# A 31-tap convolution's running sums: two channel tiles in PSUM on VectorE, the third on GpSimd, and softmax probabilities scaled on GpSimd

## The chip, the cores and the metric

The kernel runs on one core of a Trainium2 chip. The metric is the time of one execution in microseconds of the device, as the median of several runs. The core's engines run side by side, each through its own list of instructions in order: TensorE (PE in the profile; PEld is its weight load), VectorE (DVE), ScalarE (ACT), GpSimd (POOL) and SyncE (SP), which here starts the transfers.

## The reference

Two blocks of a network follow each other on 256 positions of 1024 channels, all in float32. The first has two layers with a mixer, a cross-attention to a memory of 256 rows and an MLP. The second has two layers of this form:

```python
h = x + 0.5 * swiglu(rms_norm_2(x, ffn1_norm[l]), ...)
p = rms_norm_2(h, mix_norm[l]) @ w_in[l]
u_conv, q, k, v, q_mem = jnp.split(p, splits, axis=-1)
y_conv = conv_module(u_conv, ...)        # gate, 31-tap causal convolution per channel, layer norm, silu
y_swa  = sliding_window_attention(q, k, v, swa_sinks[l])
y_mem  = memory_attention(qm, mk, mv)
h = h + jnp.concatenate([y_conv, y_swa, y_mem], axis=-1) @ w_out[l]
h = h + 0.5 * swiglu(rms_norm_2(h, ffn2_norm[l]), ...)
```

The convolution has 384 channels, each with its own 31 weights and a bias: the output at a position is the bias plus the sum over taps `j` of weight `j` times the input `30 - j` positions earlier. Every attention takes a softmax: exponentials, their sum, and each probability divided by that sum.

## The kernel before

Activations lie with 128 positions or 128 channels on the partitions. Matrix products run in float32 as three passes (`mm3`, L325 to L327): each weight tile is loaded by a transfer into `raw`, rounded by ScalarE into `hi` (L303), and the rest `raw - hi` is made by VectorE as `lo` (L304). Products add up in PSUM tiles of 128x512, which one engine at a time works on: three of tag `acc`, two of `tp` (transposes) and three of `sm` (scores).

`mixer` (L1209) is the middle of a layer of the second block. It is written as Python generators that `weave` (L388) interleaves: `conv_proj` makes the gated input of the convolution and puts it, with the channels on the partitions, into `yp` (three channel tiles `g`, 256 positions each and a border of zeros); `kv`, `qk_proj` and `vm_proj` make keys, queries and values, with rotary factors at L1195 and L1203; `mem` and `swa` are the two attentions; `taps` is the convolution, woven tap by tap with that chain; `ln` (L1427) follows it with a layer norm and the activation. `out_proj` (L479) multiplies everything with `w_out`, the convolution's three channel tiles last (the order 6, 7, 3, 4, 5, 0, 1, 2 at L1477).

In `taps` before, VectorE takes taps 0 to 16 of all three channel tiles: one multiply with bias at L1393 and sixteen multiply-adds at L1404 for each tile, in place in the SBUF tile `cv`. ScalarE takes the products of taps 17 to 30 (L1397, L1412), and GpSimd adds them in `cv2` (L1416), thirteen adds for each tile. At the end VectorE adds `cv` and `cv2` (L1420). The number of taps on VectorE is `ND` (L1565).

`softmax_ps` (L508) serves the cross-attention of the first block (L907) and both attentions of the mixer: VectorE takes the maximum (L512) and its negative times a factor (L515), ScalarE the exponentials with their sum (L525), VectorE the reciprocal (L534) and then, head by head, the scaling of the probabilities (L536). The probabilities are then transposed by TensorE (L383) into PSUM, copied by ScalarE (L909, L1335 or L1369) and multiplied with the values (L914, L1340 or L1374). A softmax of the cross-attention or of the memory attention has two heads of 128x256; of the sliding attention four and two heads of 128x128 for the first half of the positions, and three times two heads of 128x256 for the second. The factors of norms are powers taken on GpSimd (L424).

The order of each engine's instructions is not the order of the code. `list_schedule` (L128) plans it once, when the kernel is built: it takes estimated lengths (`length`, L102), the dependences and the number of buffers per tag, and gives each engine the earliest instruction in program order among those that are ready. Buffers of a tag are given out in program order. GpSimd's estimate is the same for an add and for a scaling.

## Time and profile before

| what | value |
|---|---|
| median of 3 runs | 1706.66 us (1706.2 to 1707.57) |
| the profiled execution | 1706.04 us |
| its span, first to last instruction | 1704.3 us |
| TensorE busy | 1656.1 us, 97% |
| VectorE busy | 1128.3 us, 66% |
| ScalarE busy | 941.7 us, 55% |
| GpSimd busy | 155.5 us, 9% |

The span is the profile's own clock from the first to the last instruction; the execution's time has 1.7 us around it. The two mixers of the second block, in which the convolution runs, lie at about 905 to 1019 us and 1395 to 1512 us of the span; the cross-attentions of the first block at about 160 to 215 and 460 to 520 us. A duration in a row reaches to the end of the write, so that two neighbours on one engine overlap a little: the distance from start to start is shorter than the duration.

### The profile page before, as it was taken

The numbers are of one execution on the slowest core, as the hardware profiler recorded it, in microseconds if no ns is written. First come the engines' busy times: TensorE is split into PE (matmuls) and PEld (weight loads), VectorE is DVE, ScalarE is ACT, GpSimd is POOL, SyncE is SP. The second block draws the span as 40 slices with busy tenths as digits, with TensorE's granted clock in tenths as the row PEclk, the third lists the DMA queues.
The fourth block names the chain that finished last, engine by engine and source line by source line (L and its number), as shares of the span: only waits on it lengthen the run. The fifth ranks groups of instructions, "written<-read, shape, count | busy, mean of one in ns | idle before, by whom it ended". The sixth has DMA issues, their size and how long they took to land.

```text
span 1704.3 us, 22757 instructions
## 1 busy us (share of the span) xinstructions
PE 1656.1 (97%) x8144; PEld 1399.0 (82%) x8144; DVE 1128.3 (66%) x1899; ACT 941.7 (55%) x1685; POOL 155.5 (9%) x185
## 2 busy tenths in 40 slices
PE   8999999999999999999999799999999998799998
PEld 7878888888888888888888578888888887588886
DVE  7876475556657558557558996556665559975454
ACT  7675564445666445545446674445654447664343
POOL 0120000000000000000002810000100006500000
PEclk9999999999999999999999799999999999799999
DMA  9536365565535565556455055646655554355552
GB/s 306 177 104 206 100 197 185 178 211 171 187 112 164 182 202 175 198 167 197 163 191 179 32 159 182 203 157 218 212 179 177 169 186 137 86 166 169 197 167 93
DMA packets 159393, 291.45 MB, mean 171 GB/s; under 512 B 11184, under 2 KB 36272, under 8 KB 159280
## 3 DMA queue, kind: packets, MB, share of 16 engines
q1 hardware_dynamic: 159280, 290.00, 52.6%
q8 instruction: 64, 1.05, 0.2%
q14 instruction: 49, 0.40, 0.1%
HBM read 288.91 MB, written 1.05 MB: 170 GB/s over the span
## 4 chain that ended last, share of the span: by engine, by line
PE 89%; DVE 7%; ACT 2%; issue 1%; DMA 1%; SPq 0%; POOL 0%; POOLq 0%; DVEq 0%; ACTq 0%
PE acc L327 27%; PE acc L326 27%; PE acc L325 27%; PE tp L383 4%; DVE big L1404 3%; DVE lo L304 1%; PE sm L914 1%; PE sm L901 1%; PE sm L383 1%; DVE st L555 0%; PE acc L622 0%; DVE t L536 0%; PE acc L620 0%; PE acc L621 0%; PE sm L1324 0%
## 5 line engine op out<-in xcount | busy, mean ns | idle before, releaser
L325 PE MATMUL acc<-hi,h 128*128 128x512 f32 (+1 forms) x2048 | 786.1, 384 | 1.2 <-ACT h L367 1.2
L326 PE MATMUL acc<-lo,h 128*128 128x512 f32 (+1 forms) x2048 | 783.6, 383 | 1.2 <-DVE lo L304 1.2
L327 PE MATMUL acc<-hi,h 128*128 128x512 f32 (+1 forms) x2048 | 784.5, 384 | 0.0
L304 DVE TENSOR_TENSOR lo<-raw,hi 128x1024 fp32r<-128x1024 f32 (+2 forms) x570 | 651.5, 1160 | 146.2 <-ACT hi L303 132.9
L303 ACT CAST hi<-raw 128x1024 fp32r<-128x1024 f32 (+2 forms) x570 | 564.8, 1005 | 275.0 <-PE acc L327 246.2
L325 PEld LDWEIGHTS acc<-hi,h 128*128 128x128 f32 x2048 | 385.8, 188 | 66.7 <-ACT h L367 2.1
L326 PEld LDWEIGHTS acc<-lo,h 128*128 128x128 f32 x2048 | 385.6, 188 | 65.8 <-DVE lo L304 1.8
L327 PEld LDWEIGHTS acc<-hi,h 128*128 128x128 f32 x2048 | 385.5, 188 | 64.0 <-issue 0.7
L424 POOL TENSOR_TENSOR st<-st,nhalf 128x1 f32<-128x1 f32 (+2 forms) x74 | 68.6, 929 | 1483.8 <-DVE st L429 1256.2
L367 ACT CAST h<-tp 128x512 fp32r<-128x512 f32 (+1 forms) x80 | 45.1, 563 | 151.7 <-PE tp L383 151.5
L477 DVE SCALAR_TENSOR_TENSOR x<-acc,st,x 128x512 f32<-128x512 f32 x48 | 35.9, 748 | 86.7 <-PE acc L327 86.3
L368 DVE TENSOR_TENSOR h<-tp,h 128x512 fp32r<-128x512 f32 (+1 forms) x80 | 52.9, 662 | 58.5 <-ACT h L367 58.3
L383 PE MATMUL tp<-ident,t 128*128 128x128 f32 x488 | 76.6, 275 | 13.1 <-DVE t L1157 5.9
L439 ACT ACTIVATE t<-x 128x512 f32<-128x512 f32 x56 | 35.6, 638 | 97.1 <-DVE x L477 76.7
L383 PEld LDWEIGHTS tp<-ident,t 128*128 128x128 f32 x488 | 60.2, 141 | 30.9 <-DVE t L1157 6.8
L1113 DVE TENSOR_TENSOR t<-acc,t 128x512 f32<-128x512 f32 (+1 forms) x48 | 30.9, 643 | 82.5 <-PE acc L327 82.5
L1416 POOL TENSOR_TENSOR big<-big,big 128x256 f32<-128x256 f32 x78 | 66.6, 882 | 5.1 <-ACT big L1412 5.1
L325 PE MATMUL acc<-hi,big 128*128 128x512 f32 x160 | 64.4, 403 | 0.0
L1110 ACT ACTIVATE t<-acc,st 128x512 f32<-128x512 f32 (+1 forms) x48 | 31.1, 649 | 60.0 <-PE acc L327 60.0
L326 PE MATMUL acc<-lo,big 128*128 128x512 f32 x160 | 63.6, 398 | 0.0
L1111 DVE SCALAR_TENSOR_TENSOR t<-t,acc 128x512 f32<-128x512 f32 (+1 forms) x48 | 30.7, 640 | 49.7 <-ACT t L1110 49.7
L327 PE MATMUL acc<-hi,big 128*128 128x512 f32 x160 | 63.5, 397 | 0.0
(237 smaller groups left out, 1193.0 us busy)
## 6 DMA issues: line engine op xcount, KB each, us to landing
raw<-in_ffn_w_dram SPq DMA_DIRECT2D x208, 512.0 KB, 5.1
raw<-in_mlp_w_dram SPq DMA_DIRECT2D x128, 512.0 KB, 4.8
raw<-in_ffn_w_dram SPq DMA_DIRECT2D x64, 384.0 KB, 4.1
raw<-in_xa_w_kv_dram SPq DMA_DIRECT2D x32, 512.0 KB, 5.2
raw<-in_ev_w_in_dram SPq DMA_DIRECT2D x20, 512.0 KB, 6.0
raw<-in_w_in_dram SPq DMA_DIRECT2D x24, 384.0 KB, 4.7
raw<-in_xa_w_q_dram SPq DMA_DIRECT2D x16, 512.0 KB, 5.1
raw<-in_xa_w_o_dram SPq DMA_DIRECT2D x16, 512.0 KB, 5.6
```

The costliest lines, as they stand in the source:

```text
L303: nc.scalar.copy(hi[:, :n], raw[:, :n])
L304: nc.vector.tensor_tensor(out=lo[:, :n], in0=raw[:, :n], in1=hi[:, :n].bitcast(F32), op=ALU.subtract)
L325: nc.tensor.matmul(ps, l[0], r[0], start=start, stop=False)
L326: nc.tensor.matmul(ps, l[0], r[1], start=False, stop=False)
L327: nc.tensor.matmul(ps, l[1], r[0], start=False, stop=stop)
L367: nc.scalar.copy(h, src)
L368: nc.vector.tensor_tensor(out=self.lo(k0, n, t), in0=src, in1=h.bitcast(F32), op=ALU.subtract)
L383: nc.tensor.transpose(dst[:, i * P : i * P + rows], s_, ident[:rows, :rows])
L424: nc.gpsimd.tensor_tensor(out=dst, in0=src, in1=nhalf[:, :n], op=ALU.pow)
L477: nc.vector.scalar_tensor_tensor(x_, ps, scale, x_, op0=ALU.mult, op1=ALU.add)
L1404: nc.vector.scalar_tensor_tensor(cv[:, g], yp[:, g, 2 + j : 258 + j], col(cw, 93 * l + 3 * j + g), cv[:, g], op0=ALU.mult, op1=ALU.add,)
L1416: nc.gpsimd.tensor_tensor(out=cv2[:, g], in0=cv2[:, g], in1=pj[:, g], op=ALU.add)
```

## The change

The convolution is shared out by channel tile in place of by tap. For channel tiles 0 and 1 all 31 taps run on VectorE, with the running sum in one PSUM tile `run` of tag `acc` (two tiles of 256 side by side); the last tap writes to `cv` in SBUF. For channel tile 2 ScalarE makes all 31 products (the first with the bias, straight into `cv`), and GpSimd adds thirty of them to `cv` in a row. Two products share a tile of tag `t2`, which also holds the softmaxes' tiles. The final add of VectorE is gone, and so is `ND`. In `softmax_ps` the scaling of the probabilities goes from VectorE to GpSimd. The lines after the change: L1406 first tap and L1410 other taps on VectorE, L1397 and L1401 products on ScalarE, L1402 adds on GpSimd, L536 scaling on GpSimd.

```diff
         for h in range(nh):
-            nc.vector.tensor_scalar(dst[:, h], dst[:, h], rc[:, h : h + 1], None, op0=ALU.mult)
+            nc.gpsimd.tensor_scalar(dst[:, h], dst[:, h], rc[:, h : h + 1], None, op0=ALU.mult)
...
         def taps(t):
-            cv = spare("m2hi0")
-            cv2 = spare("m2lo0")
-            for g in range(3):
-                nc.vector.tensor_scalar(
-                    cv[:, g], yp[:, g, 2:258], col(cw, 93 * l + g), col("conv_b_2", 3 * l + g),
-                    op0=ALU.mult, op1=ALU.add,
-                )
...
-                        nc.vector.scalar_tensor_tensor(
-                            cv[:, g], yp[:, g, 2 + j : 258 + j], col(cw, 93 * l + 3 * j + g),
-                            cv[:, g], op0=ALU.mult, op1=ALU.add,
-                        )
...
-            nc.vector.tensor_tensor(out=cv, in0=cv, in1=cv2, op=ALU.add)
+            cv = big()[:, 0:3]
+            run = c3(acc(), 256)
+            for j in range(31):
+                if j % 2 == 1:
+                    pj = c3(t2(), 256)
+                for g in range(3):
+                    w_ = col(cw, 93 * l + 3 * j + g)
+                    src = yp[:, g, 2 + j : 258 + j]
+                    if g == 2 and j == 0:
+                        nc.scalar.activation(
+                            cv[:, 2], src, AF.Identity, scale=w_, bias=col("conv_b_2", 3 * l + g)
+                        )
+                    elif g == 2:
+                        nc.scalar.activation(pj[:, j % 2], src, AF.Copy, scale=w_)
+                        nc.gpsimd.tensor_tensor(
+                            out=cv[:, 2], in0=cv[:, 2], in1=pj[:, j % 2], op=ALU.add
+                        )
+                    elif j == 0:
+                        nc.vector.tensor_scalar(
+                            run[:, g], src, w_, col("conv_b_2", 3 * l + g), op0=ALU.mult, op1=ALU.add
+                        )
+                    else:
+                        nc.vector.scalar_tensor_tensor(
+                            cv[:, g] if j == 30 else run[:, g], src, w_, run[:, g],
+                            op0=ALU.mult, op1=ALU.add,
+                        )
+                yield
             cvs.append(cv)
```

The planner moves instructions at three places that the prediction speaks of. The first is VectorE in the first mixer, at the softmaxes of the memory attention (`sm` scores, `t2` probabilities, `big_1733` is `cv`, `big_1694` is `yp`). Before:

```order
L534 RECIPROCAL st_1858_8739<-st_1857_8736 128x2
L1404 SCALAR_TENSOR_TENSOR big_1733_8260<-big_1694_8082,G_72,big_1733_8260 128x256
L555 TENSOR_SCALAR st_1849_8719<-st_1848_8717,st_1684_8051 128x4
L536 TENSOR_SCALAR t2_1854_8731<-t2_1854_8731,st_1858_8739 128x256 x2
L512 TENSOR_REDUCE st_1875_8846<-sm_1873_8842 128x2
L534 RECIPROCAL st_1869_8797<-st_1868_8794 128x2
L515 SCALAR_TENSOR_TENSOR st_1876_8848<-st_1875_8846,st_1849_8719 128x2
L536 TENSOR_SCALAR t2_1865_8789<-t2_1865_8789,st_1869_8797 128x256 x2
L1404 SCALAR_TENSOR_TENSOR big_1733_8260<-big_1694_8082,G_72,big_1733_8260 128x256 x6
L368 TENSOR_TENSOR h4_1862_8773<-sm_1853_8728,h4_1861_8772 128x128
L1404 SCALAR_TENSOR_TENSOR big_1733_8260<-big_1694_8082,G_72,big_1733_8260 128x256 x2
L368 TENSOR_TENSOR h4_1862_8773<-sm_1864_8786,h4_1861_8772 128x128
```

After the change (`acc_1734` is the running sum):

```order
L534 RECIPROCAL st_1855_8703<-st_1854_8700 128x2
L515 SCALAR_TENSOR_TENSOR st_1870_8779<-st_1869_8777,st_1846_8683 128x2
L1410 SCALAR_TENSOR_TENSOR acc_1734_8261<-big_1694_8082,G_72,acc_1734_8261 128x256 x2
L534 RECIPROCAL st_1865_8745<-st_1864_8742 128x2
L1410 SCALAR_TENSOR_TENSOR acc_1734_8261<-big_1694_8082,G_72,acc_1734_8261 128x256 x2
L534 RECIPROCAL st_1872_8784<-st_1871_8781 128x2
L1410 SCALAR_TENSOR_TENSOR acc_1734_8261<-big_1694_8082,G_72,acc_1734_8261 128x256 x9
L368 TENSOR_TENSOR h4_1858_8726<-sm_1850_8692,h4_1857_8725 128x128
L1410 SCALAR_TENSOR_TENSOR acc_1734_8261<-big_1694_8082,G_72,acc_1734_8261 128x256 x4
L1410 SCALAR_TENSOR_TENSOR big_1733_8260<-big_1694_8082,G_72,acc_1734_8261 128x256
L368 TENSOR_TENSOR h4_1858_8726<-sm_1860_8734,h4_1857_8725 128x128
L1410 SCALAR_TENSOR_TENSOR big_1733_8260<-big_1694_8082,G_72,acc_1734_8261 128x256
```

The scalings are gone from this list. Three reciprocals now stand close together, and behind them come the last fifteen multiply-adds of the convolution, two of which write to `cv`.

The second place is GpSimd at the end of the same mixer (`big_1734` was `cv2`, `st` are small columns). Before:

```order
L1416 TENSOR_TENSOR big_1734_8261<-big_1734_8261,big_1872_8835 128x256 x3
L1416 TENSOR_TENSOR big_1734_8261<-big_1734_8261,big_1879_8860 128x256 x3
L1223 MEMSET big_2661_12617 128x3x32
L424 TENSOR_TENSOR st_1940_9117<-st_1939_9115,nhalf_76 128x1
L424 TENSOR_TENSOR st_1951_9150<-st_1950_9148,nhalf_76 128x1
```

After the change:

```order
L1402 TENSOR_TENSOR big_1733_8260<-big_1733_8260,t2_1914_8984 128x256
L1402 TENSOR_TENSOR big_1733_8260<-big_1733_8260,t2_1915_9004 128x256
L536 TENSOR_SCALAR t2_1883_8853<-t2_1883_8853,st_1890_8879 128x128 x4
L536 TENSOR_SCALAR t2_1896_8915<-t2_1896_8915,st_1903_8935 128x128 x2
L1402 TENSOR_TENSOR big_1733_8260<-big_1733_8260,t2_1915_9004 128x256
L1223 MEMSET big_2663_12609 128x3x32
L1402 TENSOR_TENSOR big_1733_8260<-big_1733_8260,t2_1925_9043 128x256 x2
L536 TENSOR_SCALAR t2_1906_8960<-t2_1906_8960,st_1913_8980 128x256 x2
L536 TENSOR_SCALAR t2_1917_9010<-t2_1917_9010,st_1924_9030 128x256 x2
L536 TENSOR_SCALAR t2_1927_9059<-t2_1927_9059,st_1934_9079 128x256 x2
L424 TENSOR_TENSOR st_1942_9109<-st_1941_9107,nhalf_76 128x1
L424 TENSOR_TENSOR st_1953_9142<-st_1952_9140,nhalf_76 128x1
```

Before, the adds end in blocks of three and the next things are the layer norm's two powers (L424). After it, the last adds stand between scalings of the sliding attention, and six scalings of 128x256 stand between the last add and those powers.

The third place is TensorE in the first cross-attention, from the end of one projection (`acc_408`) to the product with the values (`t2_401` are the probabilities, `acc_427` is the next projection); both pieces start behind the same pass. Before:

```order
L383 MATMUL sm_400_1779<-ident_66,t2_401_1784 128x128 x2
L327 MATMUL acc_408_1813<-hi_387_1724,h4_351_1578 128x512
L383 MATMUL sm_400_1779<-ident_66,t2_401_1784 128x128 x2
L325 MATMUL acc_427_1897<-hi_366_1682,h4_345_1534 128x512
L326 MATMUL acc_427_1897<-lo_367_1683,h4_345_1534 128x512
L327 MATMUL acc_427_1897<-hi_366_1682,h4_346_1535 128x512
L325 MATMUL acc_427_1897<-hi_366_1682,h4_345_1534 128x512
L383 MATMUL tp_410_1840<-ident_66,t2_409_1838 128x128 x3
L914 MATMUL sm_400_1779<-t2_401_1784,big_223_1055 128x128
```

After the change:

```order
L327 MATMUL acc_408_1813<-hi_387_1724,h4_351_1578 128x512
L325 MATMUL acc_427_1897<-hi_366_1682,h4_345_1534 128x512
L326 MATMUL acc_427_1897<-lo_367_1683,h4_345_1534 128x512
L383 MATMUL sm_400_1779<-ident_66,t2_401_1784 128x128 x2
L327 MATMUL acc_427_1897<-hi_366_1682,h4_346_1535 128x512
L325 MATMUL acc_427_1897<-hi_366_1682,h4_345_1534 128x512
L383 MATMUL sm_400_1779<-ident_66,t2_401_1784 128x128 x2
L383 MATMUL tp_410_1840<-ident_66,t2_409_1838 128x128 x4
L326 MATMUL acc_427_1897<-lo_367_1683,h4_345_1534 128x512
L327 MATMUL acc_427_1897<-hi_366_1682,h4_346_1535 128x512
L325 MATMUL acc_427_1897<-hi_369_1688,h4_345_1534 128x512
L914 MATMUL sm_400_1779<-t2_401_1784,big_223_1055 128x128
```

The two transposes of the first head come three projection passes later, those of the second head after five passes of this piece in place of one; then four transposes and three passes stand ahead of the product L914.

## Rows read from the trace of the kernel before

**Rows 1.** the page, parts 1 and 4: engines, chain that ended last

```profile
PE 1656.1 (97%) x8144; PEld 1399.0 (82%) x8144; DVE 1128.3 (66%) x1899; ACT 941.7 (55%) x1685; POOL 155.5 (9%) x185
PE 89%; DVE 7%; ACT 2%; issue 1%; DMA 1%; SPq 0%; POOL 0%; POOLq 0%; DVEq 0%; ACTq 0%
```

**Rows 2.** windows, first mixer: us; busy PE, PEld, DVE, ACT, POOL; clock; DMA

```profile
930.00:940.00 10.00, 7.04 (x32) 5.50 (x31) 10.00 (x17) 7.44 (x16) 9.38 (x10) 0.97 0.27 80
940.00:950.00 10.00, 10.00 (x46) 8.79 (x47) 9.85 (x30) 8.48 (x18) 9.41 (x13) 0.86 0.42 132
950.00:960.00 10.00, 8.31 (x46) 6.91 (x44) 10.00 (x26) 7.94 (x19) 8.75 (x11) 1.00 0.00 1
960.00:970.00 10.00, 4.36 (x18) 2.47 (x20) 10.00 (x19) 5.54 (x17) 9.77 (x13) 0.67 0.00 0
970.00:980.00 10.00, 7.41 (x37) 5.61 (x34) 10.00 (x19) 5.98 (x19) 6.80 (x10) 0.65 0.01 2
980.00:990.00 10.00, 8.50 (x64) 6.02 (x63) 9.97 (x35) 7.67 (x26) 0.00 (x0) 1.00 0.73 201
```

**Rows 3.** groups by line, 920 to 985 us: busy us, mean ns, idle

```profile
L1416 POOL TENSOR_TENSOR big<-big,big 128x256 f32<-128x256 f32 x39 | 33.3, 882 | 2.6 <-ACT big L1412 2.6
L1404 DVE SCALAR_TENSOR_TENSOR big<-big,G,big 128x256 f32<-128x256 f32 x48 | 30.6, 674 | 0.0
L536 DVE TENSOR_SCALAR t<-t,st 128x256 f32<-128x256 f32 x8 | 4.5, 598 | 0.0
L1393 DVE TENSOR_SCALAR big<-big,G 128x256 f32<-128x256 f32 x3 | 1.1, 407 | 0.0
L1420 DVE TENSOR_TENSOR big<-big,big 128x768 f32<-128x768 f32 x1 | 0.9, 947 | 0.0
```

**Rows 4.** the same view of the second mixer, 1415 to 1480 us, VectorE

```profile
L1404 DVE SCALAR_TENSOR_TENSOR big<-big,G,big 128x256 f32<-128x256 f32 x48 | 30.5, 672 | 0.0
```

**Rows 5.** VectorE in order of time, first mixer: start us, us

```profile
923.49 2.06 DVE L1404 SCALAR_TENSOR_TENSOR big<-big,G,big 128x256 f32<-128x256 f32 x5
964.24 1.62 DVE L536 TENSOR_SCALAR t<-t,st 128x256 f32<-128x256 f32 x2
```

**Rows 6.** single lines: duration ns min/median/max

```profile
L1404 DVE SCALAR_TENSOR_TENSOR big<-big,G,big x12: 472/478/479, 923.5 to 929.0; 128x256 f32<-128x256 f32 x12
L477 DVE SCALAR_TENSOR_TENSOR x<-acc,st,x x48: 739/750/752, 288.4 to 1697.0; 128x512 f32<-128x512 f32 x48
L377 DVE SCALAR_TENSOR_TENSOR h<-tp,G,h x160: 336/342/354, 6.9 to 1515.9; 128x128 fp32r<-128x128 f32 x160
L1195 DVE TENSOR_TENSOR t<-acc,rC x12: 273/342/347, 939.7 to 1443.1; 128x192 f32<-128x192 f32 x8, 128x128 f32<-128x128 f32 x4
```

**Rows 7.** GpSimd's groups by shape, whole span

```profile
L762 POOL TENSOR_TENSOR h<-h,h 128x1024 f32<-128x1024 f32 x1 | 2.4, 2375 | 13.4 <-DVE st L504 13.4
L1425 POOL TENSOR_SCALAR hg<-G 128x3 f32<-128x3 f32 x2 | 0.5, 232 | 0.0
```

**Rows 8.** GpSimd's instructions in order of time, first mixer

```profile
961.86 8.28 POOL L1416 TENSOR_TENSOR big<-big,big 128x256 f32<-128x256 f32 x11
994.04 1.00 POOL L424 TENSOR_TENSOR st<-st,nhalf 128x1 f32<-128x1 f32 x1 [16.58 <-DVE st L1436]
```

**Rows 9.** first cross-attention, VectorE and TensorE in order of time

```profile
173.45 0.62 DVE L536 TENSOR_SCALAR t<-t,st 128x256 f32<-128x256 f32 x2
173.58 0.39 PE L325 MATMUL acc<-hi,h 128*128 128x512 f32 x1
173.80 0.40 PE L326 MATMUL acc<-lo,h 128*128 128x512 f32 x1
174.03 0.38 PE L383 MATMUL sm<-ident,t 128*128 128x128 f32 x2
174.49 0.38 PE L383 MATMUL sm<-ident,t 128*128 128x128 f32 x2
```

**Rows 10.** TensorE's waits, 915 to 1012 us: total, times, longest

```profile
PE tp L383 <- DVE t L1157: 3.0, 1, 3.0
```

21 lines of the change are left out of this document (removed).

## The prediction

> **What bounds the kernel now.** I read the busy shares and the chain that ended last first [rows 1]: TensorE is busy 97% of the span and 89% of the chain, VectorE is 7% of it. So a change on VectorE, ScalarE and GpSimd can pay only where TensorE waits, and I looked for those places in the busy time by stretches. They are the two mixers with the convolution. In the first one TensorE lacks 3.0, 0, 1.7, 5.6, 2.6 and 1.5 us in six stretches of ten from 930 to 990 us, together 14.4 us, and from 960 to 980 us its granted clock is about 0.66 of full besides [rows 2]. VectorE is full in all six, and GpSimd nearly full until the adds end. The reader is to see that VectorE, not TensorE, sets the pace there.
>
> What VectorE does with that time stands in the groups of the stretch [rows 3]: 48 multiply-adds of the convolution take 30.6 us, 674 ns each on the mean, and the second mixer shows the same, 30.5 us [rows 4]. While GpSimd has not begun its adds, the same instruction takes 478 ns [rows 6], and five of them take 2.06 us, which is one each 0.40 us as their ends overlap [rows 5]. So the multiply-adds lose a third of their time beside GpSimd, and GpSimd's adds suffer with them: 882 ns on the mean, but 0.75 us where eleven run in 8.28 us [rows 3, 8]. Instructions whose first input lies in PSUM don't stretch: L1195 runs in that same time and its largest duration is 347 ns with a median of 342 [rows 6].
>
> **The change part by part**, for one mixer.
>
> VectorE's convolution. It loses 48 multiply-adds, three first taps and the final add: 30.6 + 1.1 + 0.9 = 32.6 us [rows 3]. It gains 60 multiply-adds and two first taps. No row writes a running sum in PSUM. The nearest rows have one input in PSUM, one in SBUF and a scalar of their own per partition, as the new one has: 342 ns for 128 columns and 750 for 512 [rows 6], so between them 478 for 256. That equals the undisturbed multiply-add in SBUF, so I take its pace too, 0.40 us. Bounds: at the bottom 0.33, from L1195, which has no scalar (342 ns for 192 columns, 64 more at the slope of the two rows make 410, less the overlap of 0.08); at the top 0.48, if nothing overlaps because each sum waits for the one before. With 0.40 the new work is 60 x 0.40 + 2 x 0.40 = 24.8 us. Saved: **7.8 us**. By the bounds it is 12.0 or 3.0.
>
> One rule speaks against this step. The Trainium skill's page "VectorE: DVE Perf Modes", section "The TRN2 errata", gives a fixed cost of 58 cycles for SBUF and 120 for PSUM sources, which by its clock of 0.96 GHz would make each tap an estimated 65 ns dearer, the saving 3.9 us smaller and the time 1695.2 us. The trace doesn't agree: its instruction with a PSUM source interpolates to the same 478 ns [rows 6].
>
> The scaling of probabilities. Eight scalings of the memory attention leave VectorE's full stretch: **4.5 us** saved [rows 3]. The twelve of the sliding attention leave it too, but lie behind the full stretch, and I count nothing for them. For the softmax itself the step is a move: two scalings took 1.62 us where GpSimd was in the way [rows 5] and 0.62 where not [rows 9]. GpSimd shows a scaling only at three columns, 232 ns [rows 7]. Its add of two inputs grows by (2375 - 753) / 768 = 2.1 ns a column [rows 7, 8]; with one input I take half, 0.232 + 256 x 0.00106 = 0.50 us, and 0.37 for 128 columns. Bounds: 0.31, VectorE's own pace [rows 9], and 0.88, an add's mean here [rows 3].
>
> GpSimd's load in a mixer. It had 39 adds in 33.3 us [rows 3]. Now 30 adds x 0.75 = 22.6 us, as the multiply-adds no longer hold it up, and 14 x 0.50 + 6 x 0.37 = 9.2 us of scalings, together 31.8 us. The load hardly changes, so the queue is not the bound at these prices. But each scaling now stands in one row with the adds, and the layer norm's power L424 now stands behind six scalings of 128x256, where before it waited for VectorE alone [rows 8]. Those six are 6 x 0.50 = **3.0 us** on the convolution's last path, which out_proj ends with; I give them back in full.
>
> ScalarE's products. 42 become 31; ScalarE is below 8.5 of 10 in all those stretches [rows 2]. Nothing; if its cover went, a product would hold GpSimd's next add.
>
> The accumulation tile. The running sum holds one of three, and the projections go on with two. They alternate, so a projection starts late when the one before the last is evacuated late. The row is TensorE's wait of 3.0 us for L1157, which evacuates the second memory projection [rows 10]. It already stops TensorE there, through the transposes behind it, so a tile less stops it at the same event: I take nothing, with 3.0 us a mixer as the upper end. It should even shrink, as that chain runs through VectorE.
>
> The cross-attention. There TensorE was full, so each later softmax could cost. A pair of scalings takes 1.0 us in place of 0.62 [rows 9], but the list gives the first transposes three passes more at 0.22 us (173.58 to 173.80) and the second pair four. Started at 173.45, GpSimd's two results come at 173.95 and 174.45; the transposes would now come at about 174.7 and 175.4 [rows 9]. Cost nothing; at 0.88 each they would come at 174.3 and 175.2, still just in time, so the upper end is a few tenths for each of eight softmaxes, about 3 us in all.
>
> **The sum.** 7.8 + 4.5 - 3.0 = 9.3 us a mixer, 18.6 us for two. TensorE can use it, since it lacks 14.4 us in each. From the profiled execution's 1706.0 us (0.6 below the median of the runs) that is **1687.4 us**. With 0.33 or 0.48 us a multiply-add it would be 1679 or 1697, which is this case's own range.
>
> **The rivals.**
>
> *GpSimd becomes the bound.* If the adds stay at 0.88 although VectorE is out of their way, and a scaling costs what an add does, a mixer's load is 30 x 0.88 + 14 x 0.88 + 6 x 0.56 = 42.1 us, 8.8 more than before. For it: the adds now form one chain on one tile, so that none can start before the last is done, and each softmax waits in their queue. Against it: the 0.75 us pace, and small columns are scaled in 232 ns. What is left is 9.3 - 8.8 = 0.5 us a mixer: 1705.0 us.
>
> *The running sum in PSUM costs double (slower).* Each multiply-add reads and writes 256 columns of the same PSUM tile. If VectorE cannot do both at once there, one costs as 512 columns do, 0.75 us and less the overlap 0.67 [rows 6]. Then the convolution is 60 x 0.67 + 0.8 = 41.0 us, 8.4 more than before; less 4.5, plus 3.0, each mixer is 6.9 us longer: 1719.8 us. It decides from 0.555 us a multiply-add on, where (32.6 + 4.5 - 3.0 - 0.8) / 60 balances. For it: no row shows such an instruction. Against it: accumulating passes of TensorE go on at 0.22 us for 512 columns [rows 9], so a PSUM tile takes a sum onto each column far faster than VectorE asks.
>
> *TensorE gets all of its idle time back.* With VectorE and GpSimd out of each other's way, their other small instructions shorten too, and the chains of softmaxes and norms with them. The 14.4 us of each mixer vanish: 1677.2 us. Against it: the softmax still goes through five engine changes, and the layer norm waits on GpSimd.
>
> **How the numbers follow.** The forecast has 0.67, GpSimd as the bound 0.14, the double cost 0.10, all idle time back 0.09. About 0.2% (3.4 us) can be told from no change. Forecast and full recovery are faster by more than that; of GpSimd's case, which lies at 1705, I give 0.04 to faster, 0.08 to within and 0.02 to slower; the double cost is slower. That makes 0.80, 0.08 and 0.12. The range from 1676 to 1705 holds the forecast with its bounds, the edge of full recovery and half of GpSimd's case, and leaves out the double cost.
>
> **What would show it.** Right: multiply-adds at L1410 of about 480 ns with hardly any spread beside busy GpSimd; about 25 us for 62 of them in a mixer; adds near 0.75 us; scalings near 0.5 us; TensorE's idle time per mixer down by some 9 us, most of it between 955 and 980; the layer norm's power last on GpSimd and waited for. Wrong: multiply-adds above 0.55 us; scalings at or above 0.9 us with transposes (L383) waiting for GpSimd, in the cross-attention too; TensorE as idle as before while VectorE has gaps, which would mean that the pace was set by the chain through the engines and not by VectorE's load.

## The result and the profile after

The changed kernel takes 1715.0 us (median of four runs, 1714.1 to 1716.7), the kernel before, in runs beside it, 1706.4 us (four runs, 1705.1 to 1707.6). The ratio is 1.0051 with a 95% interval of 1.0039 to 1.0063: slower by 0.5%, some 8.6 us. The forecast was 1687.4 us. The profiled execution of the changed kernel took 1716.7 us, its span is 1714.8 us.

The page of the changed kernel, parts 1 and 4, answers to [rows 1]:

```profile
PE 1659.1 (97%) x8144; PEld 1396.1 (81%) x8144; DVE 1107.2 (65%) x1863; ACT 936.5 (55%) x1663; POOL 187.8 (11%) x223
PE 87%; POOL 4%; DVE 4%; ACT 3%; issue 2%; DMA 1%; SPq 0%; POOLq 0%; ACTq 0%; DVEq 0%
```

VectorE fell from 7% to 4% of the chain that ended last, as meant, but GpSimd rose from 0% to 4%, and TensorE's own share went down from 89% to 87%. One wait was exchanged for another. Which one, TensorE's waits by line say: total, times, longest in us; first the stretch of the first cross-attention (170 to 205 us), then the second (480 to 515 us), then the first mixer (920 to 1015 us).

```profile
PE sm L383 <- POOL t L536: 3.3, 2, 1.8
...
PE sm L383 <- POOL t L536: 1.1, 2, 0.6
...
PE sm L383 <- POOL t L536: 9.5, 8, 3.6
PE acc L325 <- DVE t L1157: 1.3, 1, 1.3
```

The transposes of the probabilities (L383) wait for the scalings on GpSimd (L536) in all three places. The wait for L1157 [rows 10] did shrink, from 3.0 to 1.3 us.

The windows: busy time of TensorE, its weight load, VectorE, ScalarE and GpSimd, then the granted clock, the DMA share and GB/s. First four windows of the two cross-attentions in the kernel before:

```profile
180.00:190.00 10.00, 10.00 (x58) 8.66 (x58) 7.70 (x15) 9.34 (x20) 0.70 (x1) 1.00 0.51 154
190.00:200.00 10.00, 10.00 (x58) 8.69 (x57) 6.93 (x12) 7.35 (x18) 0.70 (x1) 1.00 0.66 215
490.00:500.00 10.00, 10.00 (x58) 8.67 (x57) 7.32 (x12) 8.30 (x20) 1.00 (x2) 1.00 0.69 223
500.00:510.00 10.00, 10.00 (x61) 8.85 (x60) 3.83 (x9) 4.59 (x13) 0.83 (x2) 1.00 0.41 132
```

The same four in the changed kernel, then its first mixer, whose rows answer to [rows 2] but lie 7 to 8 us earlier in the program's course, since the mixer starts that much later.

```profile
180.00:190.00 10.00, 8.24 (x49) 6.82 (x48) 4.60 (x10) 6.44 (x17) 4.46 (x3) 1.00 0.51 157
190.00:200.00 10.00, 8.51 (x44) 6.89 (x43) 6.25 (x8) 6.87 (x16) 3.71 (x2) 1.00 0.53 162
490.00:500.00 10.00, 9.30 (x53) 7.71 (x52) 6.29 (x8) 8.95 (x20) 3.03 (x3) 1.00 0.60 186
500.00:510.00 10.00, 9.38 (x52) 7.44 (x52) 4.70 (x9) 6.27 (x17) 2.73 (x4) 1.00 0.62 194
...
960.00:970.00 10.00, 5.89 (x31) 4.42 (x29) 9.82 (x29) 9.43 (x29) 8.37 (x12) 0.99 0.00 1
970.00:980.00 10.00, 9.79 (x61) 7.31 (x62) 9.58 (x22) 7.43 (x19) 9.45 (x12) 0.67 0.01 2
980.00:990.00 10.00, 4.27 (x22) 2.54 (x22) 10.00 (x27) 6.29 (x23) 9.69 (x10) 0.84 0.66 180
990.00:1000.00 10.00, 9.26 (x41) 6.08 (x42) 5.30 (x23) 2.19 (x7) 6.45 (x9) 0.64 0.54 189
```

In the four stretches of the cross-attentions TensorE was full before; now it lacks 1.76 + 1.49 + 0.70 + 0.62 = 4.6 us. In the mixer it is as idle as before: it lacks 15.3 us from 930 to 1020 us, against 14.4 before, most of it from 960 on (4.1 us) and from 980 on (5.7 us). Its granted clock is 0.64 to 0.84 from 970 to 1000 us, where before it was 0.67 and 0.65 for 20 us [rows 2]. GpSimd is at 9.5 and 9.7 of 10 from 970 to 990. Of the prediction's signs of a wrong forecast one is plainly there, L383 waiting for GpSimd in the cross-attention too. The other, TensorE as idle as before while VectorE has gaps, is there by half: where TensorE lacks most, from 980 to 990, VectorE is full, and its gap from 990 on falls where TensorE lacks 0.7 us.

GpSimd's groups by shape over the whole span, and the lines of the two instructions on which the sum rested (duration ns min/median/max, first and last start, forms):

```profile
L1402 POOL TENSOR_TENSOR big<-big,t 128x256 f32<-128x256 f32 x60 | 49.5, 824 | 52.1 <-ACT t L1401 48.8
L536 POOL TENSOR_SCALAR t<-t,st 128x256 f32<-128x256 f32 x44 | 46.7, 1077 | 48.4 <-DVE st L534 37.2 <-DVE st L519 6.8 <-DVE st L447 4.3
L536 POOL TENSOR_SCALAR t<-t,st 128x128 f32<-128x128 f32 x12 | 9.7, 828 | 0.0
```

```profile
L1410 DVE SCALAR_TENSOR_TENSOR acc<-big,G,acc x116: 473/490/491, 931.0 to 1471.6; 128x256 f32<-128x256 f32 x116
L536 POOL TENSOR_SCALAR t<-t,st x56: 601/928/2832, 173.7 to 1502.3; 128x256 f32<-128x256 f32 x44, 128x128 f32<-128x128 f32 x12
L1402 POOL TENSOR_TENSOR big<-big,t x60: 720/732/1730, 930.3 to 1490.9; 128x256 f32<-128x256 f32 x60
```

The multiply-adds are what was forecast, 490 ns with no spread, where before the mean was 674 [rows 3]. The adds have their 0.73 us in the median. The scaling is the surprise: one input and one scalar a partition cost GpSimd 1077 ns on the mean for 256 columns, more than an add of two inputs (824), and up to 2.8 us. The forecast had 0.50, with 0.88 as its upper bound.

Why 2.8 us shows in order of time, GpSimd and VectorE in the first cross-attention (start us, us):

```profile
173.67 1.86 POOL L536 TENSOR_SCALAR t<-t,st 128x256 f32<-128x256 f32 x2 [4.34 <-DVE st L447]
183.19 3.74 POOL L536 TENSOR_SCALAR t<-t,st 128x256 f32<-128x256 f32 x2 [6.18 <-DVE st L534]
...
182.92 0.17 DVE L534 RECIPROCAL st<-st 128x2 f32<-128x2 f32 x1 [1.33 <-ACT t L525]
183.00 0.19 DVE L447 TENSOR_SCALAR st<-st 128x1 f32<-128x1 f32 x1
183.86 2.36 DVE L304 TENSOR_TENSOR lo<-raw,hi 128x1024 fp32r<-128x1024 f32 x2 [0.66 <-ACT hi L303]
```

Alone, two scalings take 1.86 us, 0.93 each. Beside VectorE's L304, which splits weights and reads two SBUF inputs, they take 3.74, which is 1.88 longer, and all of that falls on the second, the 2.83 us above; L304 itself keeps its 1.18 us each. The Trainium skill's page "SBUF — State Buffer", section "Who interferes with whom", says that a VectorE instruction with two SBUF inputs contends with a GpSimd instruction that reads SBUF, over ports that only one of the two holds at a time. The rows agree: the scaling ends only 0.7 us after the second split. VectorE splits weights all through the program, so a scaling on GpSimd can meet one anywhere; by the median of 0.93 us, most of them meet none.

### The profile page after: what moved, and what is told of

Read it like the earlier page. It is cut to its first block, busy times and chain, and to the rows that moved or that the text cites. A ratio compares the mean times of both kernels' runs of the same rounds, so it can differ in the third digit from the quotient of the medians.

```text
span 1714.8 us, 22744 instructions
## 1 busy us (share of the span) xinstructions
PE 1659.1 (97%) x8144; PEld 1396.1 (81%) x8144; DVE 1107.2 (65%) x1863; ACT 936.5 (55%) x1663; POOL 187.8 (11%) x223
## 4 chain that ended last, share of the span: by engine, by line
PE 87%; POOL 4%; DVE 4%; ACT 3%; issue 2%; DMA 1%; SPq 0%; POOLq 0%; ACTq 0%; DVEq 0%
PE acc L325 26%; PE acc L327 26%; PE acc L326 26%; PE tp L383 4%; POOL t L536 2%; POOL big L1402 2%; DVE lo L304 1%; ACT hi L303 1%; PE sm L914 1%; PE sm L901 1%; PE sm L383 1%; DVE acc L1410 1%; DMA raw<-in_ev_w_in_dram 0%; DMA x<-in_x_dram 0%; ACT t L525 0%
## 5 line engine op out<-in xcount | busy, mean ns | idle before, releaser
L325 PE MATMUL acc<-hi,h 128*128 128x512 f32 (+1 forms) x2048 | 786.6, 384 | 6.8 <-DVE t L1157 3.1
L304 DVE TENSOR_TENSOR lo<-raw,hi 128x1024 fp32r<-128x1024 f32 (+2 forms) x570 | 651.9, 1161 | 149.4 <-ACT hi L303 136.9
L325 PEld LDWEIGHTS acc<-hi,h 128*128 128x128 f32 x2048 | 386.0, 189 | 72.8 <-ACT t L1258 3.4
L424 POOL TENSOR_TENSOR st<-st,nhalf 128x1 f32<-128x1 f32 (+2 forms) x74 | 63.2, 856 | 1360.5 <-DVE st L429 1243.9
L383 PE MATMUL tp<-ident,t 128*128 128x128 f32 x488 | 75.3, 273 | 4.3 <-DVE t L866 3.8
L383 PEld LDWEIGHTS tp<-ident,t 128*128 128x128 f32 x488 | 60.3, 140 | 19.8 <-DVE t L866 4.2
L325 PE MATMUL acc<-hi,big 128*128 128x512 f32 x160 | 64.1, 401 | 0.0
L536 POOL TENSOR_SCALAR t<-t,st 128x256 f32<-128x256 f32 (+1 forms) x56 | 56.5, 1024 | 48.4 <-DVE st L534 37.2
```

Source lines behind the costliest of these rows:

```text
L304: nc.vector.tensor_tensor(out=lo[:, :n], in0=raw[:, :n], in1=hi[:, :n].bitcast(F32), op=ALU.subtract)
L325: nc.tensor.matmul(ps, l[0], r[0], start=start, stop=False)
L383: nc.tensor.transpose(dst[:, i * P : i * P + rows], s_, ident[:rows, :rows])
L424: nc.gpsimd.tensor_tensor(out=dst, in0=src, in1=nhalf[:, :n], op=ALU.pow)
L536: nc.gpsimd.tensor_scalar(dst[:, h], dst[:, h], rc[:, h : h + 1], None, op0=ALU.mult)
```

## The experiments

All times stand against runs of the kernel before on the same chip; the difference is between the two medians. L1404, L1416 are lines of the kernel before, L1402, L1410 of the changed one; in some of the runs the lines are shifted by two or three. The kernels without adds and the one with half the taps leave out a part of the convolution.

| run | us | against before | ratio, 95% |
|---|---|---|---|
| the changed kernel | 1715.0 | +8.6 | 1.0051, 1.0039 to 1.0063 |
| convolution alone | 1700.1 | -5.9 | 0.9966, 0.9953 to 0.9978 |
| scaling alone | 1728.6 | +22.6 | 1.0129, 1.0115 to 1.0144 |
| cross-attention's scalings back | 1708.3 | +2.4 | 1.0015, 1.0006 to 1.0024 |
| convolution alone, sums in SBUF | 1708.0 | +2.1 | 1.0011, 1.0002 to 1.0020 |
| convolution alone, two banks | 1699.4 | -7.5 | 0.9952, 0.9940 to 0.9965 |
| changed kernel, list told the price | 1714.1 | +7.2 | 1.0041, 1.0029 to 1.0054 |
| convolution alone, 8 taps to GpSimd | 1705.9 | -1.0 | 0.9991, 0.9982 to 1.0000 |
| convolution alone, 8 scalings on ScalarE | 1701.7 | -5.2 | 0.9972, 0.9960 to 0.9983 |
| convolution alone, half the taps | 1694.3 | -11.9 | 0.9929, 0.9916 to 0.9943 |
| cross-attention's back, no adds | 1694.1 | -12.1 | 0.9926, 0.9914 to 0.9939 |
| convolution alone, no adds | 1690.7 | -15.4 | 0.9909, 0.9896 to 0.9921 |
| convolution alone, list told taps' price | 1703.4 | -2.8 | 0.9981, 0.9972 to 0.9990 |

**The two halves of the change.** The convolution alone:

```
         for h in range(nh):
-            nc.gpsimd.tensor_scalar(dst[:, h], dst[:, h], rc[:, h : h + 1], None, op0=ALU.mult)
+            nc.vector.tensor_scalar(dst[:, h], dst[:, h], rc[:, h : h + 1], None, op0=ALU.mult)
```

> The convolution as changed, the scaling of probabilities back on VectorE. Theory (the scaling on GpSimd eats the gain): VectorE's 62 convolution instructions took 29.3 us in the changed kernel's first mixer against 32.6 before (30.6 + 1.1 + 0.9), and the scalings beside them go at 0.31 to 0.56 us each; so 3 to 5 us a mixer are won, 1696 to 1701 us in all, TensorE full again from 180 to 200 and 490 to 510 us. Rival (the convolution's new order is the cause: one chain of 30 adds over 31 steps, an accumulation tile less, ScalarE's products late): no gain, 1706 to 1712 us, with TensorE as idle in the mixers as in the changed kernel (15 us each).

1700.1 us, 5.9 less than before: the theory's value, and faster. The cross-attentions are full again (20.00 of 20 us from 180 and from 490). The convolution's new form is not the cause of the loss.

The scaling alone is the reverse: the kernel before with that one line on GpSimd.

> The convolution as before, only the scaling of probabilities on GpSimd. Theory: the cross-attentions lose what they lose in the changed kernel, about 5 us; in a mixer GpSimd has 39 adds (33.3 us) and 20 scalings (18 us at 0.93 each), over 51 us where TensorE's stretch is 60 us, and the transposes wait; VectorE is relieved of 4.5 us; so 2 to 9 us more a mixer, 1715 to 1729 us. Rival (the scaling costs nothing or helps, the convolution is the cause): VectorE's 4.5 us a mixer are won, 1697 to 1706 us.

1728.6 us, 22.6 more, at the theory's upper end. The scaling costs more beside the old convolution than beside the new one (8.6 + 5.9 = 14.5). The old one gives GpSimd 39 adds a mixer and not 30, and VectorE's taps there read two SBUF inputs; which of the two weighs more, no run separates. Its windows show GpSimd full for 20 us, and TensorE's clock low (us; busy PE, PEld, DVE, ACT, POOL; clock; DMA):

```profile
970.00:980.00 10.00, 4.09 (x15) 2.17 (x16) 10.00 (x19) 6.62 (x19) 10.00 (x10) 0.54 0.00 0
980.00:990.00 10.00, 8.15 (x38) 5.62 (x37) 9.45 (x15) 4.61 (x11) 10.00 (x11) 0.78 0.79 232
```

**Where the scaling costs.** In the changed kernel the cross-attention's call gets VectorE back, the mixers' keep GpSimd:

```
-    def softmax_ps(ps, dst, nh, n, cs, extra=None):
+    def softmax_ps(ps, dst, nh, n, cs, extra=None, on=nc.gpsimd):
...
-            nc.gpsimd.tensor_scalar(dst[:, h], dst[:, h], rc[:, h : h + 1], None, op0=ALU.mult)
+            on.tensor_scalar(dst[:, h], dst[:, h], rc[:, h : h + 1], None, op0=ALU.mult)
...
-                softmax_ps(c3(psc, 256), c3(pr_, 256), 2, 256, cs)
+                softmax_ps(c3(psc, 256), c3(pr_, 256), 2, 256, cs, on=nc.vector)
```

> As the changed kernel, but the cross-attention's scalings (16 of 56) are back on VectorE; those of the mixers stay on GpSimd. Theory: TensorE gets back the 4.6 us that it lost from 180 to 200 and from 490 to 510 us, and no more: 1709 to 1711 us, so that what is left above the kernel before, some 4 us, belongs to the mixers and the start. Rival (the lag ahead of the first mixer has another cause): 1714 to 1716 us.

2.4 us over before, so the cross-attention's 16 scalings cost 8.6 - 2.4 = 6.2 us. I had expected at most the 4.6 us that the windows show as idle. The difference of 1.6 is within what the two intervals leave open, but the traces side with the larger figure: the first multiply-add of the first mixer starts at 931.0 us in the changed kernel, here at 922.5, at 923.9 in the convolution alone and at 923.5 before, so that 7 to 8.5 us are lost ahead of the mixers. Idle time is here only the lower end of what the waits cost. The 40 scalings of the mixers cost the rest, 2.4 + 5.9 = 8.3 us.

**The price, or the list's wrong idea of it?** The list that orders the instructions reckoned 678 ns for a scaling. Told about 917:

```
     if e == ENG.Pool:
         if getattr(op, "op", None) == ALU.pow:
             return 300 + 164 * n
+        if len([x for x in ins if free(x) > 1]) == 1:
+            return 2.45 * n + 290
         return 2.1 * n + 140
```

> The changed kernel, whose list is now told what a scaling on GpSimd costs: 2.45 ns a column and 290 ns (917 ns for 256 columns) instead of 2.1 and 140 (678). Nothing else differs. Theory (the price itself and the one queue with the adds make the loss): the list can put other passes ahead of the late transposes, but GpSimd's work stays; 1707 to 1714 us, TensorE still waiting for scalings in the mixers. Rival (the list, planning with too low a price, put the transposes too early, and that is the loss): 1698 to 1702 us, near the run with the convolution alone.

1714.1 us, not to be told from the changed kernel. TensorE's waits for scalings shrink from 23.6 to 16.2 us in the whole span, but the time does not follow. So the list's low price was not the cause.

**The price, or the queue with the adds?** Two kernels without GpSimd's 30 adds a mixer, one with the mixers' scalings on GpSimd, one with them on VectorE:

```
-                        nc.gpsimd.tensor_tensor(
-                            out=cv[:, 2], in0=cv[:, 2], in1=pj[:, j % 2], op=ALU.add
-                        )
```

> As the run with the cross-attention's scalings back on VectorE and the mixers' on GpSimd (1708.3 us), but GpSimd's 30 adds of the convolution in each mixer are left out, so that part of the convolution is missing. To be held against the next run, the same with all scalings on VectorE: with the adds, that pair differs by 8.2 us. If the scalings cost because they stand in one queue with the adds: 0 to 2 us between the pair. If their own price (0.91 us for 256 columns, more beside VectorE's work on SBUF) does: 5 to 9 us.

> As the run with the convolution alone (1700.1 us), but GpSimd's 30 adds of the convolution in each mixer are left out, so that part of the convolution is missing. GpSimd is busy 8.4 of 10 at most there and waits for ScalarE's products; if its adds lie beside VectorE's work and cost nothing: 1698 to 1701 us. If they hold VectorE up, or the layer norm behind the last of them: 1692 to 1697 us.

The pair lies at -12.1 and -15.4: 3.3 us apart, where with the adds it is 8.3. So neither value that I had written down: of the mixers' loss about 5 us come from sharing GpSimd with the adds, about 3 from the scaling's own price. Four medians stand behind this split, so it can be off by 2 us or more. How that sharing looks in the changed kernel, GpSimd in order of time (start us, us):

```profile
967.93 5.44 POOL L536 TENSOR_SCALAR t<-t,st 128x256 f32<-128x256 f32 x6
973.34 10.76 POOL L1402 TENSOR_TENSOR big<-big,t 128x256 f32<-128x256 f32 x11
984.08 2.84 POOL L536 TENSOR_SCALAR t<-t,st 128x256 f32<-128x256 f32 x2
986.89 2.39 POOL L1402 TENSOR_TENSOR big<-big,t 128x256 f32<-128x256 f32 x2
989.26 4.96 POOL L536 TENSOR_SCALAR t<-t,st 128x128 f32<-128x128 f32 x6
```

There is no gap in it from 967.93 to 994.2. The adds held up by six scalings come in one block of 10.8 us. The next two scalings start when it ends, at 984.08; their reciprocal was there at 983.6, so the queue costs them 0.5 us, and two of VectorE's L304 beside them as much again for each (1.42 us in place of 0.93). Of the sliding attention's six, four had their reciprocals at 987.1 and start at 989.26, behind those two and two more adds. So here the adds are delayed more than the scalings, and the rows of this stretch don't add up to the 5 us.

The second kernel of the pair shows something that I had not looked for: without the adds the convolution alone gains another 9.5 us, more than either value. The reason behind the second value holds, the adds hold VectorE up. VectorE's softmax steps in the first mixer (groups by shape, 920 to 985 us: busy us, mean ns), the convolution alone and then without the adds:

```profile
L536 DVE TENSOR_SCALAR t<-t,st 128x256 f32<-128x256 f32 x8 | 3.8, 521 | 0.0
L515 DVE SCALAR_TENSOR_TENSOR st<-st,st 128x2 f32<-128x2 f32 x4 | 0.9, 228 | 0.0
```

```profile
L536 DVE TENSOR_SCALAR t<-t,st 128x256 f32<-128x256 f32 x10 | 3.1, 347 | 0.0
L515 DVE SCALAR_TENSOR_TENSOR st<-st,st 128x2 f32<-128x2 f32 x4 | 0.6, 156 | 0.0
```

In the kernel before the same two took 598 ns [rows 3] and 475 ns on the mean. Each of them stands in a softmax's chain for which TensorE waits. How much of the 9.5 us is this stretching, how much the queue (the layer norm's and the heads' power L424 and the rotary adds L1207 stand in it too) and how much the list's other order, these runs do not separate.

**What the multiply-adds cost, and why.** In the changed kernel and in the convolution alone, taps that follow each other start 0.52 us apart, not 0.40. Sums in SBUF:

```
-            run = c3(acc(), 256)
+            run = cv
```

> As the run with the convolution alone, but the two running sums lie in SBUF (in the tile that receives the result) and the accumulation tile stays with the projections. If the place of the sums is what spares the two engines each other: multiply-adds beside busy GpSimd again 0.67 us on the mean, 60 of them 40 us, and adds 0.88; 8 to 12 us a mixer more than with the sums in PSUM, so 1715 to 1725 us. If the place does not matter: the time of that run, 1696 to 1701 us. On the pace of taps that follow each other: 0.52 us each in PSUM in the changed kernel (six in 3.11 us) against 0.40 before; if the place makes the difference, taps away from GpSimd's work go at 0.40 here; if the order does (the same channel tile comes round every second tap, not every third), 0.52.

1708.0 us lies between the two: the place, with the accumulation tile that goes back to the projections, matters by 8 us, less than I had thought, because a tap beside GpSimd's adds costs 573 ns on the mean (1002 at most) and not 670. Two banks instead of one:

```
-            run = c3(acc(), 256)
+            run = [acc()[:, 0:256], sm()[:, 0:256]]
```

(and `run[g]` for `run[:, g]`)

> As the run with the convolution alone (1700.1 us), but its two running sums lie in two PSUM banks instead of one: one in an accumulation tile, one in a tile of the scores, of which two are left. There, taps that follow each other start 0.52 us apart in one bank (six in 3.12 us), 0.40 us in SBUF (six in 2.45 us with GpSimd idle). If writing and reading the same bank in turn is what spaces them, taps here go at 0.40 and up to 60 x 0.12 = 7 us a mixer are won, less what a scores tile less costs: 1688 to 1698 us. If it is PSUM as such, they stay at 0.52 and the time is 1700 us or some us more for the tile.

The pace, VectorE in order of time, the convolution alone, then the sums in SBUF while GpSimd was idle, then two banks (L1406 is the first tap of a sum):

```profile
922.72 1.13 DVE L1406 TENSOR_SCALAR acc<-big,G 128x256 f32<-128x256 f32 x2
923.89 3.12 DVE L1410 SCALAR_TENSOR_TENSOR acc<-big,G,acc 128x256 f32<-128x256 f32 x6
```

```profile
967.34 2.45 DVE L1410 SCALAR_TENSOR_TENSOR big<-big,G,big 128x256 f32<-128x256 f32 x6
```

```profile
924.62 0.54 DVE L1406 TENSOR_SCALAR sm<-big,G 128x256 f32<-128x256 f32 x1
925.07 0.48 DVE L1410 SCALAR_TENSOR_TENSOR acc<-big,G,acc 128x256 f32<-128x256 f32 x1
925.46 0.49 DVE L1410 SCALAR_TENSOR_TENSOR sm<-big,G,sm 128x256 f32<-128x256 f32 x1
925.85 0.49 DVE L1410 SCALAR_TENSOR_TENSOR acc<-big,G,acc 128x256 f32<-128x256 f32 x1
926.25 0.48 DVE L1410 SCALAR_TENSOR_TENSOR sm<-big,G,sm 128x256 f32<-128x256 f32 x1
```

(3.12 - 0.48) / 5 = 0.53 in one bank, (2.45 - 0.47) / 5 = 0.40 in SBUF, 0.39 in two banks. It is the shared tile that spaces them, not PSUM and not the order of the channel tiles. In the shared tile each tap starts 35 ns after the one before has ended (35 to 36 in all 66 pairs of the changed kernel), and the trace notes with each a wait for VectorE's own semaphore, the counter by which an instruction waits for an earlier one. Taps in two tiles carry such waits too, but start before the one just ahead has ended. And the second sum's first tap, which touches nothing that the first sum's wrote, carries a wait in one tile and none in two (the pairs of L1406 start 0.58 and 0.45 us apart). So what spaces them is, as far as the traces show, a wait that the program makes for the tile; whether the bank would space them without it, no run shows.

The time is 1699.4 us, 7.5 less than before; against the convolution alone that is 1.6 us, within the intervals. Only taps that follow each other gain: each counted to its end or to VectorE's next start, the 62 instructions of the first mixer hold VectorE for 27.3 us in one bank and for 25.0 in two, so that 2.3 us a mixer were taken off it, and not 60 x 0.12 = 7. And the scores have a tile less: TensorE now waits 8.6 us for scalings (L536) in the first mixer, where the convolution alone has 2.7. What VectorE's time is worth can't be read from this run.

**Does VectorE's load set the pace at all?** Half of the multiply-adds left out:

```
-                    else:
+                    elif j < 15 or j == 30:
                         nc.vector.scalar_tensor_tensor(
                             cv[:, g] if j == 30 else run[:, g], src, w_, run[:, g],
```

> As the run with the convolution alone (1700.1 us), but 30 of the 60 multiply-adds on VectorE of a mixer are left out (taps 15 to 29 of two channel tiles), so that part of the convolution is missing; nothing else is. VectorE has 30 x 0.52 = 15.6 us less in each mixer. TensorE lacks 12.1 us in the first mixer (920 to 1020 us) and 11.5 in the second there. If VectorE's load sets the pace of the mixers, nearly all of that comes back: 1676 to 1682 us. If the chains through the engines do (in two banks 60 x 0.12 = 7 us a mixer less gave 1699.4 us, next to nothing): 1692 to 1700 us.

1694.3 us: 6.0 us less, the chains' value. Counted as above, the taps hold VectorE for 14.5 us a mixer in place of 27.3, so this is for some 26 us of its work. (The list orders what is left anew, which this run does not hold apart.) In order of time, GpSimd's adds, VectorE and then TensorE around the first softmaxes of that kernel:

```profile
953.18 6.65 POOL L1402 TENSOR_TENSOR big<-big,t 128x256 f32<-128x256 f32 x6
```

```profile
957.87 0.15 DVE L515 SCALAR_TENSOR_TENSOR st<-st,st 128x2 f32<-128x2 f32 x1
957.94 0.68 DVE L512 TENSOR_REDUCE st<-sm 128x2 f32<-128x512 f32 x1
958.54 0.70 DVE L304 TENSOR_TENSOR lo<-raw,hi 128x512 fp32r<-128x512 f32 x1
959.16 0.68 DVE L515 SCALAR_TENSOR_TENSOR st<-st,st 128x2 f32<-128x2 f32 x1
959.76 0.68 DVE L512 TENSOR_REDUCE st<-sm 128x2 f32<-128x512 f32 x1
960.83 0.69 DVE L555 TENSOR_SCALAR st<-st,st 128x4 f32<-128x4 f32 x1 [0.39 <-POOL st L424]
961.43 0.15 DVE L534 RECIPROCAL st<-st 128x2 f32<-128x2 f32 x1
961.56 0.16 DVE L515 SCALAR_TENSOR_TENSOR st<-st,st 128x2 f32<-128x2 f32 x1
961.63 1.62 DVE L536 TENSOR_SCALAR t<-t,st 128x256 f32<-128x256 f32 x2
```

```profile
957.88 1.13 PE L1361 MATMUL sm<-big,t 128*128 128x256 f32 x4 [0.84 <-DVE t L1311]
962.60 0.66 PE L383 MATMUL sm<-ident,t 128*128 128x128 f32 x2 [3.60 <-ACT t L525]
```

No tap is left here, and TensorE still waits 3.6 us. The row puts this down to a later softmax's exponentials (L525), which end at 962.49; the first scaling ends at almost the same time, 962.45. The softmax begun at 957.87 has its exponentials at 959.3 and its scaling only at 961.63. Ahead of its reciprocal in VectorE's queue stand two more maxima, a weight split, and a factor that waits for GpSimd's power. Small steps take 0.68 us where alone they take 0.15 to 0.22: the L515 begun at 959.16 ends at 959.84, just as GpSimd's last add of the row ends. And the scalings take 1.62 for two. VectorE is full because the list fills it with what is ready, and being full does not say that its load is the bound.

Waiting is not the whole price either. After TensorE has idled, its granted clock drops for some us from the upper level (2.4 GHz) to the lower (1.2 GHz), as from 970 on in the changed kernel. In both mixers together (900 to 1035 and 1390 to 1535 us, one profiled execution each), TensorE is idle for 27.9 us before, 23.5 in the convolution alone, 22.2 with half the taps and 18.4 without the adds; it works at the lower level for 25.8, 18.7, 11.7 and 12.7 us. Half of that is an estimate of what the clock costs, which differs between executions of one kernel too. By it, half the taps gain 1.3 us of waiting and 3.5 of clock against the convolution alone, the adds left out 5.1 and 3.0. In the kernel with the scaling alone, whose clock is low for longest, it is 5.9 and 8.3 us more than before.

**Three tries at a better one.** The last 4 of 31 taps of both channel tiles as products on ScalarE and adds on GpSimd (with a final add):

```
-                    else:
+                    elif j < NV:
...
+                k = j // 3 if j % 3 == 2 else len(more)
+                if k < len(more):
+                    g, i = more[k]
...
+                        nc.gpsimd.tensor_tensor(
+                            out=cv2[:, g], in0=cv2[:, g], in1=px[:, g], op=ALU.add
+                        )
```

> As the run with the convolution alone, but the last 4 of 31 taps of the two channel tiles on VectorE go to ScalarE (products) and GpSimd (6 more adds a mixer); a final add on VectorE joins the parts. VectorE, busy 9.7 of 10 in most stretches of the mixers there, loses 8 x 0.52 and gains 2 x 0.48 = 3.2 us a mixer. If VectorE's load still sets the pace: 1692 to 1697 us. If the chain through the engines does (ScalarE's products, GpSimd's adds, the norm behind the last sum): 1699 to 1703 us.

1705.9 us, worse than both values: some 3 us less on VectorE and 6 adds more on GpSimd in each mixer cost 5 us in all. It fits the run without adds, by which GpSimd's work is the dearer of the two; ScalarE's products and the tiles for them came along, and are not held apart.

The memory attention's scalings on ScalarE:

```
+                nc.scalar.activation(dst[:, h], dst[:, h], AF.Copy, scale=rc[:, h : h + 1])
```

> As the run with the convolution alone, but the 8 scalings of a mixer's memory attention go to ScalarE (a copy with a scale), where a product of the same size takes 0.41 us in a row. VectorE is relieved of 8 x 0.45 = 3.6 us a mixer, ScalarE gains 3.3. If moving the scaling off VectorE is worth while and only GpSimd was the wrong place for it: 1693 to 1698 us. If ScalarE, at 8.4 to 8.7 of 10 from 950 to 960 us, makes the transposes later: 1700 to 1704 us.

1701.7 us, the second value, and not to be told from the convolution alone. TensorE now waits for ScalarE's scalings (2.3 us in the first mixer).

The list told the taps' true distance (520 ns for 397):

```
     if e == ENG.DVE:
         big = [x for x in ins if free(x) > 1]
...
+        if psum and n == 256 and len(ins) > len(big) == 2:
+            return 520
```

> As the run with the convolution alone (1700.1 us), but the list is told that a multiply-add with its sum in PSUM takes 520 ns instead of 397. The work is the same. If the list's low price puts VectorE's softmax steps too far behind the taps: 1694 to 1698 us. If the order hardly depends on it: 1698 to 1703 us.

1703.4 us, just above the second value: no gain. So of all that was run with the whole convolution computed, the convolution alone (1700.1) and its form with two banks (1699.4) are the best, both faster than the kernel before and the changed one; between the two the runs don't decide.

## Why the prediction was wrong, step by step

**The scaling of probabilities** is the step that failed. "with one input I take half, 0.232 + 256 x 0.00106 = 0.50 us". Alone it is 0.93 us, with VectorE's weight splits beside it up to 2.83, 1.08 on the mean. Half of an add's slope was an inference from the number of inputs, and the nearest row of the same operation, 232 ns for three columns [rows 7], said nothing of the slope. The upper bound of 0.88 was an add's mean, and I took for granted that one input could not cost more than two. The Trainium skill's page "GPSIMD Engine Reference", section "Engine selection", calls one-input work roughly line-rate there; the runs show the contrary for a scaling with a scalar of its own in each partition, 0.93 us against 0.73 for the add of two inputs. In the sum the scaling stood as -4.5 + 3.0 = -1.5 us a mixer; measured it is +8.3 us for the two mixers, so that 11.3 us of the error lie here. The 3.0 were for the layer norm's queue alone; that the softmaxes and the adds delay each other stood at nothing.

**"Cost nothing" for the cross-attention** failed by 6.2 us. At 0.88 the transposes would have been "just in time"; that reckoning had a scaling begin when VectorE's had begun and run undisturbed. What it left out is the contention with L304, which the kernel before shows for GpSimd's adds and VectorE's taps alike, and which I had used as an argument for the convolution but not against the scaling.

**VectorE's convolution** was right in the mechanism, wrong in the size, and wrong in what VectorE's time is worth beyond that. Right: multiply-adds of 490 ns without spread, adds at 0.73 us beside them in the median. The fixed cost for PSUM sources of the Trainium skill's page "VectorE: DVE Perf Modes", section "The TRN2 errata", from which the prediction estimated a tap 65 ns dearer, is not borne out: 490 ns here and 478 in SBUF, and in two banks the same pace as in SBUF. Mis-sized: "I take its pace too, 0.40 us" measured 0.52 for taps that follow each other, since both sums share a tile. That is the case of the upper bound, in which each waits for the one before, and 0.04 more than its 0.48. Counted from start to start, the 62 instructions come to 28.0 us a mixer (27.3 in the convolution alone) instead of 24.8, and those of the kernel before to 30.6; the forecast's 32.6 were durations, which overlap. So 2.6 to 3.3 us a mixer were saved and not 7.8, and this alone takes most of the 15.6 us of that step down to the 5.9 that came. Wrong besides: "TensorE can use it, since it lacks 14.4 us in each". Half the taps away give 6.0 us for some 26. A full VectorE was read as the bound. What the rows show in its place is the chain of softmaxes through VectorE's and GpSimd's queues, for the waits that were followed; not every wait was.

**The adds** were costed at their pace and at nothing else. Beside the new convolution they are worth 9.5 us of the time, although GpSimd had 0% of the chain that ended last before [rows 1].

**ScalarE's products** at nothing: nothing in these runs speaks against it. **The accumulation tile** at nothing against the kernel before holds too: TensorE's waits for L1157 and L1307 in the first mixer were 3.7 us and are 2.3 in the changed kernel. But the tile is not free. These waits now stand at the projections (L325), which is where a missing tile shows, and with the sums in SBUF they are 1.0.

**The rivals.** "GpSimd becomes the bound" came nearest, with the queue and the scaling that costs what an add does, and with the sign that showed it (scalings at 0.9 us, L383 waiting for GpSimd, in the cross-attention too). Its time of 1705.0 was too low, because it still credited the convolution and VectorE's relief in full and set nothing for the cross-attention. (Its 0.56 us for a scaling of 128 columns stands in no row; the shortest measured was 0.60.) "The running sum costs double" was wrong: 0.52 us stays below its threshold of 0.555. So the changed kernel is slower, but not for the reason of the rival that forecast a slower one. "TensorE gets all of its idle time back" was wrong as well: even without the adds 18.4 of the mixers' 27.9 us are left.

Put together: 1706.4 - 5.9 for the convolution + 6.2 for the cross-attentions + 8.3 for the mixers = 1715.0. The parts are differences of the runs, so they add up by construction, and the scaling alone (22.6) shows that they depend on each other. Of the 27.6 us between forecast and result the mixers' scalings have 11.3, the convolution 15.6 - 5.9 = 9.7, the cross-attentions 6.2, and 0.4 lies in the run that the sum started from.

## What to carry to other kernels

Before work moves to GpSimd, look for a row of the very operation at the very size; with none, bound it above by more than its two-input neighbour, and add once more the time of whatever two-input work VectorE may be doing at that moment. An engine that is full is not yet the bound: take a piece of its work away, as in the run with half the taps, or follow one late result back through the queues, and count how much of its waiting was for its own inputs and how much for its turn. An engine with a small share of the busy time can still be dear, if its queue, or what it holds up on other engines, lies on a chain that is waited for.

## What the runs showed of the hardware

Two running sums in one PSUM tile: multiply-adds on VectorE start 0.53 us apart, each after the end of the one before, with a wait for VectorE's own semaphore; in two banks they start 0.39 apart, in SBUF 0.40, all with a duration of 0.47 to 0.49 us for 256 columns. GpSimd's scaling by a scalar per partition: 0.93 us for 256 columns of 128 partitions, its shortest for 128 columns 0.60, dearer than its add of two inputs (0.73 for 256). A softmax step on VectorE of two columns, with two SBUF inputs, took 0.15 us alone and 0.68 beside GpSimd's adds: small instructions lose most, as they end with the other engine's instruction. After idling, TensorE worked at the lower clock level for 11.7 to 42.4 us of the two mixers, depending on the kernel.
